# Seven small edits to a two-layer trunk kernel: decay broadcasts with 128 rows, the state chain's priority, later transposes, block-wise products, early low halves, and a shorter rstd chain

## Chip, cores and metric

One core of one Trainium2 chip. The metric is the device time of one launch in microseconds (us): the median of 3 runs, 939.8 for the kernel before (937.92 to 940.81).

## What is computed

x (512 tokens by 1024, float32) goes through two layers, each with a norm ahead of and behind it:

```python
def rmsnorm(x, g):
    return x * lax.rsqrt(jnp.mean(x * x, -1, keepdims=True) + EPS) * g

def ssd_fox_layer(x, ...):                      # layer 0
    proj = rmsnorm(x, g_pre) @ w_in
    z, xbc, dt_raw, q, k, v, f_raw = jnp.split(proj, ...)
    xbc = silu(causal_depthwise_conv(xbc, conv_w, conv_b))
    y = ssd_chunked(xs, softplus(dt_raw + dt_bias), a, bm, cm) + xs * d_skip
    yg = y * silu(z_ssd)                        # 4 groups, each normed for itself
    y = yg * lax.rsqrt(jnp.mean(yg * yg, -1, keepdims=True) + EPS) * ssd_norm
    o = forgetting_attention(q, k, v, log_sigmoid(f_raw + fgate_b)) * silu(z_fox)
    out = concatenate([y, o]) @ w_out
    return x + rmsnorm(out, g_post)

def conformer_conv_layer(x, ...):               # layer 1
    val, gate, z = jnp.split(rmsnorm(x, g_pre) @ w_in, 3, -1)
    h = causal_depthwise_conv(val * sigmoid(gate), conv_w, conv_b)   # width 31
    h = silu(layernorm(h, ln_g, ln_b)) * silu(z)
    return x + rmsnorm(h @ w_out, g_post)
```

`ssd_chunked` works on chunks of 128 tokens. Within a chunk it needs, for each of 16 heads, the decay matrix exp(cs[l] - cs[s]) under the diagonal, where cs is a running sum; between chunks a state H is carried: H = H * decay + new.

## The kernel before

The 512 tokens lie in four blocks of 128 (`NB`), the 1024 channels in eight slices of 128 (`KT`). Every product is made in three passes in a rounded float32 format: both factors are split into a high and a low half, and high x high, high x low and low x high are summed in one PSUM bank (`mm3`, or three `mm` in a row). Names with h and l at the end (`uh`, `ul`, `hlh`, `hll`) are such halves.

The work is a list of `Job`s, one for each weight tile of 128 x 1024 values. A job's weights are loaded on SyncE's queue (L163), cast on ScalarE (L157, L159) and their low half is made on VectorE or GpSimd (L191). Then `run` makes the job's products in eight chunks (a few have more). Between chunks it lets `Steps.chunk` put in steps of the state space part and of the attention: each step has a name, what it needs, and a delay in estimated microseconds (`DL`) after that. So **TensorE's order is fixed by hand**, when the program is built. On the other engines a scheduler sets the order by priority; `tc.high_priority(offset=HP)` pulls a piece of code ahead.

Part of layer 1's low halves is made ahead, during layer 0: `early` is a generator over 52 of layer 1's jobs. For each it loads the weights (`pre`, L202), casts them on ScalarE in two halves (`prh`, L211), subtracts on VectorE (`pre`, L212) and writes the low half to memory (`lo`, L216), all on the same queues. `run` advances it at each 8th chunk of jobs 5 to 12, each 7th from job 26, and each 11th from job `JO` = 56, where layer 0's output projection begins; `J1` = 72 is layer 1's first job. What isn't done by then is drained afterwards.

The places that the change touches:

- `rstd_of` (L344) makes var = ss/n + EPS on VectorE (L346) and rstd = var^-0.5 on GpSimd (L348). `sumsq` (L355) is the sum of squares, on ScalarE. `scaled` (L358) norms a block: two sums of squares, an addition (L364), rstd, and two products (L367); its result `u` is transposed on TensorE (`uT`, L106).
- `z_ssd` and `v_proj` are the products of the gate and of the attention's values: for each k a loop over the token blocks (bank names `tm`).
- the output projection (bank `o`, `first` and `second` for the two halves of 512 columns), and `finish` for each block: the sum of squares of the second half, a product with the gain (L710), the sum of both halves' squares (L711), rstd, and x + y * rstd (L714).
- the decay broadcasts: `seg` multiplies a selector, one column broadcast to 128, by the running sums `cs2` and so spreads one head's row over 128 partitions (`bc`). There are 16, four in each group. `cs2` has 48 rows: the high half in rows 0 to 15, the low half in rows 32 to 47, the rest zero.
- the state chain: `states` (the three states H of a group, L1313 and L1314) and `state_parts` (their halves, `hlh` and `hll` out of `H`, L119), which the products with the state (`yo`) need.
- `to_yT`: the transposes of a group's normed y (`yT`, L106). They come `DL[11]` after `gate_scale`, which scales y by its rstd (L1388). `cv` (L528) is the short convolution's steps, on VectorE too.

Of the kernel before, what the change touches and what calls it, by code (L numbers as in the profile page):

```python
# [15 lines left out]
P = 128  # L16
# [20 lines left out]
def trunk(  # L37
# [292 lines left out]
    def run(n, after=None):  # L330

        for _ in range(n):
            for c, _ in enumerate(chunks()):
                if after is not None:
                    after()
                i = state["run"]
                if 5 <= i < 13 or 26 <= i:
                    if (8 * i + c) % (11 if i >= JO else 7 if i >= 26 else 8) == 0:
                        next(early, None)
# [4 lines left out]
    def rstd_of(ss, n):  # L344
        v = col("var", ss.shape[-1])
        V.tensor_scalar(v, ss, 1.0 / n, EPS, ALU.mult, ALU.add)  # L346
# [10 lines left out]

    def scaled(dst, xs):  # L358

        s2 = col("s2", 2)  # L360
        for i, t in enumerate(xs):
            sumsq(t, s2[:, i : i + 1])
        if len(xs) == 2:
            V.tensor_tensor(s2[:, 0:1], s2[:, 0:1], s2[:, 1:2], ALU.add)  # L364
        r = rstd_of(s2[:, 0:1], D)
# [175 lines left out]
    def z_ssd(ch):  # L541
        pbs = []

        def go(k2, wh, wl):
            if k2 == 0:
                pbs.extend(bank("tm") for _ in range(NB))
            for j in range(2):
                k = 2 * k2 + j
                for b in range(NB):
# [13 lines left out]
    def v_proj(ch):  # L563
        pbs = []

        def go(k4, wh, wl):
            if k4 == 0:
                pbs.extend(bank("tm") for _ in range(2))
            for j in range(4):
                k = 4 * k4 + j  # L570
                for b in range(NB):
# [60 lines left out]
    def out_proj(w, stages, nk, gpost, resid, done, hooks):  # L632
# [27 lines left out]
        def first(k2, wh, wl):  # L660
# [4 lines left out]
            for j in range(2):  # L665
                k = 2 * k2 + j
                for b in range(NB):
# [3 lines left out]
                    if k == nk - 1:  # L671
                        t = t2("o0")
                        s0.append(sumsq(pb0[b]))
# [33 lines left out]
        def finish(b):  # L707
            ss = sumsq(pb1[b])
            y1 = [o0[b], t2("y1")]
            V.tensor_tensor(y1[1], pb1[b], gpost[1], ALU.mult)  # L710
            V.tensor_tensor(ss, ss, s0[b], ALU.add)  # L711
            r = rstd_of(ss, D)
# [485 lines left out]
    cs2 = cp.tile([48, S], F32R, name="cs2")  # L1198
    sel2 = cp.tile([48, 16], F32R, name="sel2")
# [3 lines left out]
    V.tensor_tensor(sel2, ident[0:48, 0:16], ident[0:48, 32:48], ALU.add)  # L1203
# [32 lines left out]
    DL = [2, 7, 4, 11, 4, 9, 4, 9, 9, 3, 3, 6]  # L1236
# [62 lines left out]
    def states(g):  # L1299
# [6 lines left out]
        H = S_["H"] = [t2("H") for _ in range(2)]  # L1306
        for c in range(3):
            h = q256(H, c)
            if c == 0:
                A.copy(h, q256(st, 0))  # L1310
            else:
                dec = cdec[:, 4 * g : 4 * g + 4, c].unsqueeze(2).to_broadcast([P, 4, 64])
                V.tensor_tensor(h4(h), h4(q256(H, c - 1)), dec, ALU.mult)  # L1313
                V.tensor_tensor(h, h, q256(st, c), ALU.add)  # L1314

    def state_parts(g):
        H = SG[g]["H"]
        r = []
        for i, w in enumerate((512, 256)):
# [282 lines left out]
```

## Time and profile before

| what | value |
|---|---|
| median of 3 runs | 939.8 us |
| the profiled execution | 940.86 us |
| its span, first to last instruction | 939.1 us |
| mean granted TensorE clock | 0.993 |
| TensorE busy | 906.6 us (97% of the span), 4683 matmuls |
| VectorE, ScalarE, GpSimd busy | 731.1, 605.3, 511.6 us |
| moved by DMA | 166.14 MB, mean 177 GB/s |

The profile shows one execution. A row of the timeline has the start, the duration, the engine (PE is TensorE, DVE VectorE, ACT ScalarE, POOL GpSimd, SPq SyncE's queue), the line, the operation, the tiles out<-in and their shape, how many rows were put together (x2), and in brackets how long the engine sat idle before it and whom it waited for. Matmuls are pipelined: each begins before the one before it has ended, so their pace is read from start to start. 128*128 ahead of a shape means rows times columns of the stationary operand. A group of a tile has count, then ns shortest/median/longest. A row of the windows has the stretch, its length, busy us (and instructions) of PE, PEld, DVE, ACT and POOL, the granted clock, the DMA share and GB/s.

### The profile page before, as it was taken

To read this page: it belongs to the slowest core of one execution; us is meant where nothing else is said; L and a number is where in the kernel's file an instruction comes from. 1 tells how busy PE (TensorE), PEld (TensorE's weight loads), DVE (VectorE), ACT (ScalarE), POOL (GpSimd) and SP (SyncE) were. 2 spreads that over 40 slices of the span, in tenths; PEclk is the share of its full clock that TensorE was granted. 3 is DMA by queue.
4 is the path that set the end of the run, shared out by engine and by line. 5 is a ranking of instruction groups with operands and counts; after the bars stand their busy time and mean duration, and the time that the engine had idled before them with its cause. 6 is when DMAs were issued, how large, how long until landed. Compare 5 with 4: busy or idle time off the path is not lost.

```text
span 939.1 us, 13909 instructions
## 1 busy us (share of the span) xinstructions
PE 906.6 (97%) x4683; PEld 755.6 (80%) x4683; DVE 731.1 (78%) x1284; ACT 605.3 (64%) x1134; POOL 511.6 (54%) x476
## 2 busy tenths in 40 slices
PE   6999999998999999989899989999999999999997
PEld 6887787787798888778678879888888887787885
DVE  5667968788977887988877347899999999979502
ACT  5757667576855767677575536987886877658300
POOL 2604554535633444445573111998999999847310
PEclk9999999999999999999999999999999999999999
DMA  7725631347765574674538986546564665554503
GB/s 208 229 77 180 202 90 53 104 128 237 241 202 159 163 243 158 182 244 150 168 110 285 333 301 227 169 157 213 180 209 150 190 197 174 157 157 155 182 1 112
DMA packets 182507, 166.14 MB, mean 177 GB/s; under 512 B 7900, under 2 KB 151908, under 8 KB 182436
## 3 DMA queue, kind: packets, MB, share of 16 engines
q1 hardware_dynamic: 182420, 165.25, 54.9%
q8 instruction: 37, 0.61, 0.3%
q14 instruction: 34, 0.28, 0.1%
q10 hardware_dynamic: 16, 0.00, 0.0%
HBM read 133.64 MB, written 31.46 MB: 176 GB/s over the span
## 4 chain that ended last, share of the span: by engine, by line
PE 42%; DVE 6%; DMA 5%; issue 2%; ACT 2%; SPq 1%; POOL 1%; DVEq 0%; POOLq 0%; ACTq 0%
PE m L102 29%; PE o L102 10%; DMA lo<-pre 3%; DVE pre L212 2%; DMA wr<-in_o_w_in_dram 1%; PE acc L102 1%; PE tm L102 1%; DMA wr<-in_e_w_out_dram 1%; DVE w L191 1%; PE s L102 1%; DVE pl L119 1%; PE pT L106 0%; DMA pre<-in_o_w_in_dram 0%; ACT pr L95 0%; DMA pre<-in_o_w_out_dram 0%
## 5 line engine op out<-in xcount | busy, mean ns | idle before, releaser
L102 PE MATMUL m<-uh,w 128*128 128x512 f32 (+1 forms) x1392 | 453.5, 393 | 0.0
L102 PEld LDWEIGHTS m<-uh,w 128*128 128x128 f32 x1392 | 261.4, 190 | 50.9 <-issue 3.1
L102 PE MATMUL m<-ul,w 128*128 128x512 f32 (+1 forms) x696 | 267.7, 385 | 0.0
L191 POOL TENSOR_TENSOR w<-wr,w 128x512 fp32r<-128x512 f32 x112 | 158.8, 1442 | 160.3 <-ACT w L159 123.6
L984 DVE SCALAR_TENSOR_TENSOR acc<-h,cw,acc 128x490 f32<-128x490 f32 (+13 forms) x274 | 179.0, 731 | 2.7 <-ACT acc L976 2.0
L891 POOL TENSOR_TENSOR acc<-acc,prod 128x507 f32<-128x507 f32 (+9 forms) x124 | 159.6, 1289 | 8.2 <-ACT prod L877 0.7
L102 PEld LDWEIGHTS m<-ul,w 128*128 128x128 f32 x696 | 132.3, 190 | 21.5 <-issue 0.5
L102 PE MATMUL o<-w,hlh 128*128 128x512 f32 x448 | 142.2, 399 | 2.3 <-ACT pr L95 2.3
L212 DVE TENSOR_TENSOR pre<-pre,prh 128x512 fp32r<-128x512 f32 x104 | 90.6, 889 | 44.8 <-ACT prh L211 44.6
L102 PEld LDWEIGHTS o<-w,hlh 128*128 128x128 f32 x448 | 83.4, 191 | 19.0 <-ACT pr L95 3.0
L102 PE MATMUL tm<-w,uh 128*128 128x256 f32 (+1 forms) x384 | 91.7, 330 | 1.9 <-ACT pr L95 0.9
L211 ACT CAST prh<-pre 128x512 fp32r<-128x512 f32 x104 | 61.2, 622 | 48.5 <-DMA pre<-in_o_w_in_dram 14.6
L1464 POOL TENSOR_SCALAR pr<-pr,ri 128x128 f32<-128x128 f32 (+1 forms) x64 | 39.7, 621 | 92.6 <-DVE ri L1463 85.8
L159 ACT CAST w<-wr 128x1024 fp32r<-128x1024 f32 x72 | 74.8, 1048 | 23.0 <-DMA wr<-in_e_w_in_dram 6.6
L102 PE MATMUL o<-w,hll 128*128 128x512 f32 x224 | 88.0, 393 | 0.0
L877 ACT ACTIVATE prod<-h,cw 128x507 f32<-128x507 f32 (+9 forms) x124 | 79.0, 709 | 0.0
L348 POOL TENSOR_TENSOR rstd<-var,mhalf 128x1 f32<-128x1 f32 (+1 forms) x20 | 14.0, 698 | 114.6 <-DVE var L346 114.6
L157 ACT CAST w<-wr 128x1024 fp32r<-128x1024 f32 x56 | 57.2, 1050 | 18.5 <-DMA wr<-in_o_w_out_dram 10.3
L102 PEld LDWEIGHTS tm<-w,uh 128*128 128x128 f32 x384 | 62.9, 190 | 7.6 <-DVE QS L605 1.1
L102 PE MATMUL tm<-w,ul 128*128 128x256 f32 (+1 forms) x192 | 61.2, 319 | 0.0
L95 ACT ACTIVATE pr<-s,nmx 128x128 f32<-128x128 f32 (+1 forms) x64 | 34.0, 531 | 38.0 <-DVE nmx L1458 27.8
L102 PEld LDWEIGHTS o<-w,hll 128*128 128x128 f32 x224 | 42.6, 190 | 9.0
(270 smaller groups left out, 1594.3 us busy)
## 6 DMA issues: line engine op xcount, KB each, us to landing
wr<-in_e_w_in_dram SPq DMA_DIRECT2D x56, 512.0 KB
lo<-pre SPq DMA_DIRECT2D x52, 512.0 KB
pre<-in_o_w_in_dram SPq DMA_DIRECT2D x48, 512.0 KB
wr<-in_o_w_in_dram SPq DMA_DIRECT2D x48, 512.0 KB
w<-lo SPq DMA_DIRECT2D x48, 512.0 KB
wr<-in_e_w_out_dram SPq DMA_DIRECT2D x16, 512.0 KB
wr<-in_o_w_out_dram SPq DMA_DIRECT2D x16, 512.0 KB
x<-in_x_dram SPq DMA_DIRECT2D x12, 256.0 KB
```

Of the source, the lines that this page charges most:

```text
L95: i = A.activation(*a, **kw)
L102: T.matmul(o, l, r, start=start, stop=stop, skip_group_check=True)
L157: last_cast[0] = A.copy(hi, src).ins
L159: last_cast[0] = A.copy(hi, src).ins
L191: j.eng.tensor_tensor(hl[1][i][:, sl], src[:, sl], f32(hl[0][i])[:, sl], ALU.subtract)
L211: A.copy(h[:, sl], t[:, sl])
L212: V.tensor_tensor(t.bitcast(F32R)[:, sl], t[:, sl], f32(h)[:, sl], ALU.subtract)
L348: mark["rstd"] = G.tensor_tensor(r, v, mhalf.to_broadcast([P, ss.shape[-1]]), ALU.pow).ins
L877: A.activation(prs[i][:, s:], hs[j][:, : S - s], AF.Copy, scale=w31(30 - s, j))
L891: G.tensor_tensor(a2[j][:, s:], a2[j][:, s:], prs.pop(i)[:, s:], ALU.add)
L984: V.scalar_tensor_tensor(a[:, s:], h[:, : S - s], w31(30 - s, j), a[:, s:], ALU.mult, ALU.add)
L1464: G.tensor_scalar(p[:, :L], p[:, :L], ri, 1.0, ALU.mult, ALU.mult)
```

## The change

1. `cs2` and `sel2` have 128 rows, the added ones zeros; the broadcast matmul uses all 128.
2. `states` and `state_parts` are pulled ahead by `high_priority`.
3. `DL[11]`, the delay ahead of a normed group's transposes, is 9 instead of 6.
4. `z_ssd`, `v_proj` and the first job of layer 0's output projection loop over token blocks outside and over k inside (`v_proj` by pairs of blocks).
5. `early` is advanced at each 7th chunk from job 26 to 69, and no more behind that.
6. In `scaled` and `finish` the first half's share of var, ss0/n + EPS, is made ahead (`part_var`), so that one instruction makes var out of the second sum of squares; in `finish` rstd is started before the product with the gain.

```diff
-                if 5 <= i < 13 or 26 <= i:
-                    if (8 * i + c) % (11 if i >= JO else 7 if i >= 26 else 8) == 0:
+                if 5 <= i < 13 or 26 <= i < J1 - 2:
+                    if (8 * i + c) % (7 if i >= 26 else 8) == 0:
                         next(early, None)
...
-    def rstd_of(ss, n):
+    def rstd_of(ss, n, pre=None):
         v = col("var", ss.shape[-1])
-        V.tensor_scalar(v, ss, 1.0 / n, EPS, ALU.mult, ALU.add)
+        if pre is None:
+            V.tensor_scalar(v, ss, 1.0 / n, EPS, ALU.mult, ALU.add)
+        else:
+            V.scalar_tensor_tensor(v, ss, 1.0 / n, pre, ALU.mult, ALU.add)
...
+    def part_var(ss, n):
+        p = col("pre")
+        V.tensor_scalar(p, ss, 1.0 / n, EPS, ALU.mult, ALU.add)
+        return p
...
-        s2 = col("s2", 2)
-        for i, t in enumerate(xs):
-            sumsq(t, s2[:, i : i + 1])
-        if len(xs) == 2:
-            V.tensor_tensor(s2[:, 0:1], s2[:, 0:1], s2[:, 1:2], ALU.add)
-        r = rstd_of(s2[:, 0:1], D)
+        pre = part_var(sumsq(xs[0]), D)
+        r = rstd_of(sumsq(xs[1]), D, pre)
...
-            for j in range(2):
-                k = 2 * k2 + j
-                for b in range(NB):
+            for b in range(NB):
+                for j in range(2):
+                    k = 2 * k2 + j
...
-            for j in range(4):
+            for b2 in range(2):
+              for j in range(4):
                 k = 4 * k4 + j
-                for b in range(NB):
+                for b in (2 * b2, 2 * b2 + 1):
...
-            for j in range(2):
-                k = 2 * k2 + j
-                for b in range(NB):
+            stagger = k2 == 0 and len(stages) == 1
+            for j, b in ((j, b) for b in range(NB) for j in range(2)) if stagger else ((j, b) for j in range(2) for b in range(NB)):
+                    k = 2 * k2 + j
...
-                        s0.append(sumsq(pb0[b]))
+                        s0.append(part_var(sumsq(pb0[b]), D))
...
             ss = sumsq(pb1[b])
+            r = rstd_of(ss, D, s0[b])
             y1 = [o0[b], t2("y1")]
             V.tensor_tensor(y1[1], pb1[b], gpost[1], ALU.mult)
-            V.tensor_tensor(ss, ss, s0[b], ALU.add)
-            r = rstd_of(ss, D)
...
-    cs2 = cp.tile([48, S], F32R, name="cs2")
-    sel2 = cp.tile([48, 16], F32R, name="sel2")
+    cs2 = cp.tile([P, S], F32R, name="cs2")
+    sel2 = cp.tile([P, 16], F32R, name="sel2")
...
-    DL = [2, 7, 4, 11, 4, 9, 4, 9, 9, 3, 3, 6]
+    DL = [2, 7, 4, 11, 4, 9, 4, 9, 9, 3, 3, 9]
...
-        H = S_["H"] = [t2("H") for _ in range(2)]
+        with tc.high_priority(offset=HP):
+            H = S_["H"] = [t2("H") for _ in range(2)]
...
-        for i, w in enumerate((512, 256)):
-            r.append(hilo(H[i][:, :w], w))
+        with tc.high_priority(offset=HP):
+            for i, w in enumerate((512, 256)):
+                r.append(hilo(H[i][:, :w], w))
...
-        mm(bc, sel2[:, h : h + 1].to_broadcast([48, P]), cs2, True, True)
+        mm(bc, sel2[:, h : h + 1].to_broadcast([P, P]), cs2, True, True)
```

How the order on the engines moves is shown at three places. First TensorE, at the transposes of group 2 (`yT`), before:

```order
L102 MATMUL m_2289<-uh_138,w_2186 128x512
L102 MATMUL m_2289<-ul_146,w_2186 128x512
L102 MATMUL m_2289<-uh_138,w_2186 128x512
L106 MATMUL yT_2299<-ident,y_1809 128x128 x2
L106 MATMUL yT_2299<-ident,y_1837 128x128 x2
L102 MATMUL m_2289<-uh_139,w_2186 128x512
```

and after, at the end of the same job's 24 matmuls:

```order
L102 MATMUL m_2297<-uh_145,w_2194 128x512
L102 MATMUL m_2297<-ul_153,w_2194 128x512
L102 MATMUL m_2297<-uh_145,w_2194 128x512
L106 MATMUL yT_2349<-ident,y_1814 128x128 x2
L106 MATMUL yT_2349<-ident,y_1833 128x128 x2
L102 MATMUL m_2367<-uh_138,w_2252 128x512
```

The job that stands as m_2289 before and as m_2297 after has 24 matmuls: the transposes stood behind its third and now stand behind its last, 21 matmuls later. In group 3 they move by 12.

Second, VectorE in front of those transposes, before:

```order
L346 TENSOR_SCALAR var_2207<-ss_2198 128x4
L212 TENSOR_TENSOR pre_2313<-pre_2313,prh_2428 128x512
L528 SCALAR_TENSOR_TENSOR cv_2177<-m_2101,c_136,cv_2177 128x509
L1388 TENSOR_SCALAR y_1809<-y_1809,rstd_2209 128x256 x2
L1388 TENSOR_SCALAR y_1837<-y_1837,rstd_2209 128x256
L528 SCALAR_TENSOR_TENSOR cv_2239<-m_2182,c_136,cv_2239 128x511
L1388 TENSOR_SCALAR y_1837<-y_1837,rstd_2209 128x256
```

and after:

```order
L347 TENSOR_SCALAR var_2230<-ss_2221 128x4
L212 TENSOR_TENSOR pre_2272<-pre_2272,prh_2356 128x512
L533 SCALAR_TENSOR_TENSOR cv_2243<-m_2190,c_136,cv_2243 128x511
L1395 TENSOR_SCALAR y_1814<-y_1814,rstd_2232 128x256
L533 SCALAR_TENSOR_TENSOR cv_2243<-m_2190,c_136,cv_2243 128x510
L1395 TENSOR_SCALAR y_1814<-y_1814,rstd_2232 128x256
L533 SCALAR_TENSOR_TENSOR cv_2243<-m_2190,c_136,cv_2243 128x509
L1395 TENSOR_SCALAR y_1833<-y_1833,rstd_2232 128x256 x2
```

Between var and the last scaling of y stood two convolution steps; now there are three, and two of them lie between the scalings. Ahead of the first group's decays and state chain, one pair of early subtractions (`pre`) fewer stands now; the low halves of the state (`hll` out of `H`) still follow those of the decays (`hll` out of `seg`).

Third, VectorE at the end of layer 0, where the last block's x is made and normed for layer 1, before:

```order
L710 TENSOR_TENSOR y_1329_6195<-o_1258_5902,x_5662 128x512
L711 TENSOR_TENSOR ss_6192<-ss_6192,ss_5881 128x1
L212 TENSOR_TENSOR pre_6102<-pre_6102,prh_6247 128x512
L346 TENSOR_SCALAR var_6198<-ss_6192 128x1
L212 TENSOR_TENSOR pre_6102<-pre_6102,prh_6247 128x512
L714 SCALAR_TENSOR_TENSOR o_1248_5880<-o_1248_5880,rstd_6200,x_6070 128x512
L714 SCALAR_TENSOR_TENSOR y_1329_6195<-y_1329_6195,rstd_6200,x_6071 128x512
```

and after:

```order
L349 SCALAR_TENSOR_TENSOR var_6228<-ss_6225,pre_5921 128x1
L717 TENSOR_TENSOR y_1350_6232<-o_1282_5954,x_5688 128x512
L719 SCALAR_TENSOR_TENSOR o_1266_5917<-o_1266_5917,rstd_6230,x_6120 128x512
L719 SCALAR_TENSOR_TENSOR y_1350_6232<-y_1350_6232,rstd_6230,x_6121 128x512
L364 TENSOR_SCALAR pre_6245<-ss_6242 128x1
L349 SCALAR_TENSOR_TENSOR var_6250<-ss_6247,pre_6245 128x1
L372 TENSOR_SCALAR u_6240<-o_1266_5917,rstd_6252 128x512
L372 TENSOR_SCALAR u_6241<-y_1350_6232,rstd_6252 128x512
```

The two early subtractions (`pre` out of `prh`) are gone from this place, and var stands ahead of the product y. (The `pre` of 128x1 is `part_var`'s result.)

More of the change, by code (lines that the diff above doesn't have):

```diff
@@ L1202, in trunk @@
     V.tensor_copy(cs2[32:48, :], f32(csl)[0:16, :])
-    V.tensor_tensor(sel2, ident[0:48, 0:16], ident[0:48, 32:48], ALU.add)
+    V.tensor_tensor(sel2, ident[:, 0:16], ident[:, 32:48], ALU.add)
     tk = cp.tile([P, NB, P], F32, name="tk")
@@ L1305, in states @@
             mm3(q256(st, c), Bth[:, tok(c)], Btl[:, tok(c)], eh, el, True, True)
-        H = S_["H"] = [t2("H") for _ in range(2)]
[L1307 to L1314, printed above, removed]
+        with tc.high_priority(offset=HP):
+            H = S_["H"] = [t2("H") for _ in range(2)]
+            for c in range(3):
+                h = q256(H, c)
+                if c == 0:
+                    A.copy(h, q256(st, 0))
+                else:
+                    dec = cdec[:, 4 * g : 4 * g + 4, c].unsqueeze(2).to_broadcast([P, 4, 64])
+                    V.tensor_tensor(h4(h), h4(q256(H, c - 1)), dec, ALU.mult)
+                    V.tensor_tensor(h, h, q256(st, c), ALU.add)
     def state_parts(g):
```

## The prediction

> **What bounds the kernel now.** I read the page first, then the waits of TensorE, then its timeline at the places where the waits lie. The page's first lines:
>
> ```profile
> span 939.1 us, 13909 instructions
> PE 906.6 (97%) x4683; PEld 755.6 (80%) x4683; DVE 731.1 (78%) x1284; ACT 605.3 (64%) x1134; POOL 511.6 (54%) x476
> ```
>
> TensorE is busy for 97% of the span, so nothing that shortens another engine counts unless a TensorE wait goes with it, or TensorE's own work gets shorter. Its waits (us in total, times, longest):
>
> ```profile
> PE uT L106 <- DVE u L367: 2.8, 1, 2.8
> PE yT L106 <- DVE y L1388: 2.6, 2, 1.6
> PE o L102 <- ACT pr L95: 2.5, 4, 0.9
> PE yo L102 <- DVE hll L119: 2.0, 2, 1.6
> PE s L102 <- ACT pr L95: 1.5, 2, 0.8
> ```
>
> The change can win back little more than these rows, the slow clock that follows a wait, and whatever TensorE does badly while it counts as busy. For the last, the starts in the timeline matter, not the durations, since matmuls overlap. Around one decay broadcast:
>
> ```profile
> 145.26 0.40 PE L102 MATMUL m<-uh,w 128*128 128x512 f32 x1
> 145.59 0.49 PE L102 MATMUL bc<-cs,sel 48*128 48x512 f32 x1
> 146.01 0.50 PE L102 MATMUL m<-uh,w 128*128 128x512 f32 x1
> 146.34 0.40 PE L102 MATMUL m<-ul,w 128*128 128x512 f32 x1
> 146.58 0.40 PE L102 MATMUL m<-uh,w 128*128 128x512 f32 x1
> ```
>
> Start to start: 0.33 into the broadcast, 0.42 out of it, 0.33 to the next, then 0.24. Undisturbed, a 512-column matmul starts 0.23 after the one before it: the fourth interval here has just recovered, and two that are counted in one row last 0.62 where one lasts 0.39 (the rows at 567.24 and 220.99 further on). The first three intervals hold 0.33 + 0.42 + 0.33 - 3 x 0.23 = 0.39 too much.
>
> **The decay broadcasts with 128 rows.** The new rows are zeros, so the columns that stream (512) stay the same, and the evacuation reads the same bank. What must be judged is whether the 48 rows are what costs. A matmul that also leaves rows out, in the attention:
>
> ```profile
> 420.18 0.34 PE L102 MATMUL s<-KS,QS 128*128 128x384 f32 x1
> 420.36 0.34 PE L102 MATMUL s<-KX,QX 68*128 68x384 f32 x1
> 420.54 0.23 PE L102 MATMUL s<-maskq,identb 128*128 128x128 bf16 x1
> ```
>
> From 128 rows to 68 takes 0.18 and back 0.18, which is the pace for 384 columns (384/512 x 0.23 = 0.17). [...]
>
> ```profile
> L102 PE MATMUL bc<-cs,sel 48*128 48x512 f32 x16 | 7.9, 492 | 0.0
> ```
>
> Sixteen broadcasts x 0.39 = **6.2**. The two intervals next to the broadcast alone would give 16 x 0.29 = 4.6. [...]
>
> **State chain ahead.** The wait at the first group's products with the state:
>
> ```profile
> 107.59 0.28 PE L102 MATMUL yo<-hlh,hlh 128*128 128x256 f32 x1
> 109.47 0.39 PE L102 MATMUL yo<-hll,hlh 128*128 128x256 f32 x1 [1.60 <-DVE hll L119]
> ...
> 102.58 1.76 DVE L212 TENSOR_TENSOR pre<-pre,prh 128x512 fp32r<-128x512 f32 x1
> 107.66 3.17 DVE L119 TENSOR_TENSOR hll<-H,hlh 128x512 fp32r<-128x512 f32 x2
> ```
>
> The low half of the state starts at 107.66 and TensorE waits 1.60 here, 2.0 in all by the row above. In the changed order it still stands behind the four low halves of the decays, with two early subtractions among them as before; a pair of early subtractions that stood ahead of them is gone from the place, between 2 x 0.69 (a row below) and 2 x 1.76. But TensorE reaches its products 4 x 0.39 = 1.6 sooner, because of the group's four broadcasts, and only in part do the decays come sooner with it. I take half, **1.0**; ends 0 and 2.0.
>
> **Normed group's transposes later.** Group 2:
>
> ```profile
> 220.99 0.39 PE L102 MATMUL m<-uh,w 128*128 128x512 f32 x1
> 222.99 0.76 PE L106 MATMUL yT<-ident,y 128*128 128x128 f32 x3 [1.61 <-DVE y L1388]
> 224.70 0.33 PE L106 MATMUL yT<-ident,y 128*128 128x128 f32 x1 [0.95 <-DVE y L1388]
> 226.02 0.78 PE L102 MATMUL m<-uh,w 128*128 128x512 f32 x1
> ...
> 229.43 0.63 PE L102 MATMUL m<-uh,w 128*128 128x512 f32 x2
> ...
> 223.29 0.74 DVE L528 SCALAR_TENSOR_TENSOR cv<-m,c,cv 128x511 f32<-128x511 f32 x1
> ```
>
> Waits 1.61 + 0.95 = 2.56. Between 226.02 and 229.43 eight matmuls start, which is 3.41 where 8 x 0.23 = 1.84, so a half-speed clock costs another 1.57; together 4.1. The order puts the transposes 21 matmuls later, 21 x 0.23 = 4.8. VectorE's scaling now has one convolution step more in front of its last instruction, 0.74, so 2.56 + 0.74 = 3.3 must be covered and 4.8 is there. I take **4.0**; ends 2.0 (the chain a further 3.6 late) and 4.1. [...] The rows show half speed straight behind both waits, so I count it.
>
> In group 3 the transposes move 12 matmuls, 2.7, and the two low halves of a weight now stand ahead of its rstd on GpSimd:
>
> ```profile
> L191 POOL TENSOR_TENSOR w<-wr,w x112: 1276/1302/2762, 24.2 to 896.6; 128x512 fp32r<-128x512 f32 x112
> ```
>
> That is 2 x 1.3 = 2.6 against 2.7. There was no wait there before, so I allow **-1.0** for this and for other new short waits; ends 0 and -2.0.
>
> **Early low halves ended sooner, rstd chain shorter.** At the end of layer 0:
>
> ```profile
> 557.05 0.69 DVE L212 TENSOR_TENSOR pre<-pre,prh 128x512 fp32r<-128x512 f32 x1 [4.75 <-ACT prh L211]
> 557.66 0.15 DVE L346 TENSOR_SCALAR var<-ss 128x1 f32<-128x1 f32 x1
> ...
> 562.67 2.29 PE L106 MATMUL uT<-ident,u 128*128 128x128 f32 x14 [2.81 <-DVE u L367]
> 564.61 1.20 PE L102 MATMUL o<-w,hlh 128*128 128x512 f32 x2
> ...
> 567.24 0.62 PE L102 MATMUL o<-w,hlh 128*128 128x512 f32 x2
> ```
>
> In front of var stood an early subtraction that waited for its cast and its load: 4.75 + 0.69 lost on the chain that ends in u. With the 52 early jobs done before, the chain starts about 5.4 sooner and has 2.81 to cover. Also gone is the slow clock behind it: 6 matmuls from 564.61 to 567.24 take 2.63 instead of 1.38, 1.25. Together **4.1**; next late is the residual's load, which now has no early store behind it. Ends 2.8 and 4.7 (the transposes run slowly too). The early steps before that come closer together in the output projection (each 7th chunk, not each 11th): four of the 52 jobs move ahead, 4 x 1.05 MB, at
>
> ```profile
> 530.00:545.00 15.00, 15.00 (x68) 12.42 (x67) 3.35 (x6) 5.76 (x12) 0.00 (x0) 1.00 0.95 335
> ```
>
> 335 GB/s and a share of 0.95 that makes 12.5 later for whatever is queued behind. The last weight was cast at 524.5 and used at 539.8, 15.3 of cover:
>
> ```profile
> L159 ACT CAST w<-wr x6: 1046/1048/1055, 500.6 to 524.5; 128x1024 fp32r<-128x1024 f32 x6
> 539.76 0.62 PE L102 MATMUL o<-w,hlh 128*128 128x512 f32 x2
> ```
>
> So nothing, and at most a wait of 3 if the stores delay the queue by another 6. In the attention (waits of 2.5 and 1.5 above, behind the exponentials on ScalarE), there is one more pair of early casts in the order, while the staggered first job gives the exponentials room: I take **+1.0**, ends -2 and +4 (all of both rows).
>
> At the very end:
>
> ```profile
> 933.82 0.15 DVE L346 TENSOR_SCALAR var<-ss 128x1 f32<-128x1 f32 x1
> 934.12 0.55 POOL L348 TENSOR_TENSOR rstd<-var,mhalf 128x1 f32<-128x1 f32 x1 [6.29 <-DVE var L346]
> 934.70 0.75 DVE L714 SCALAR_TENSOR_TENSOR o<-o,rstd,x 128x512 f32<-128x512 f32 x1 [0.72 <-POOL rstd L348]
> ```
>
> Until now the post-norm product (0.69) and the addition (0.15) stand ahead of var. When var goes first, rstd runs beside the product: **0.8** off the tail. The start has the same shorter chain, but there the next weights set the pace, so I count 0. The products taken block by block change no count of matmuls, and they free banks one by one: 0.
>
> **The sum.** 6.2 + 1.0 + 4.0 + 4.1 + 1.0 + 0.8 - 1.0 = 16.1. The profiled execution took 940.86, of which the span is 939.1 and 1.8 lies outside it; the median of the runs is 939.8. I go from 940.3, midway: **924.2**.
>
> **The rivals.**
>
> *Rows don't matter* (the broadcast operand costs). The broadcasts keep their 6.2: 924.2 + 6.2 = 930.4. For it: the stationary stays a broadcast of one column. Against it: the interval before the broadcast is long too. Chance 0.10.
>
> *The attention is bound by VectorE and ScalarE.* Time won before it is lost again in waits for banks, and only the boundary and the tail stay, 4.1 + 0.8: 940.3 - 4.9 = 935.4. For it: the two rows on pr. Against it: 1.5 + 2.5 is little, and TensorE would have to wait three times as much there. Chance 0.13.
>
> *Slower: the block order asks for weights too early.* With the token block outside, the second k of a gate job's weight tile is needed after 3 matmuls, not after 12: 9 x 0.23 = 2.1 sooner. The value jobs need their fourth k 18 half-width matmuls sooner, again 2.1. If each of the 16 jobs waits for that, 16 x 2.1 = 33 is lost: 924.2 + 33 = 957; from 8 such jobs on (8 x 2.1 = 16.8) the gain is gone. Tightest is the first of these jobs:
>
> ```profile
> 45.10 0.62 PE L102 MATMUL tm<-w,uh 128*128 128x512 f32 x2
> 42.47 2.98 POOL L191 TENSOR_TENSOR w<-wr,w 128x512 fp32r<-128x512 f32 x2 [0.53 <-ACT w L159]
> ```
>
> GpSimd ends at 45.45, the low half is needed at about 46. For the others no TensorE wait names a weight. Chance 0.03.
>
> *The state chain isn't ahead:* its 1.0 is lost, 925.2; a case inside the forecast, 0.1 of its chance.
>
> **How the numbers follow.** The forecast has 0.70, the rivals 0.10, 0.13 and 0.03; 0.04 is left for other losses that bring it to no change. The range reaches up to 936, over the first two rivals, and down to 917: with every term at its better end (6.2 + 2.0 + 4.1 + 4.7 + 4.0 + 0.8, no allowance) the sum is 21.8, 918.5, and one more stretch of slow clock as long as the 1.57 above, behind a wait of the attention, may go too. About 0.3% (2.8) can be told from no change; 935.4 is beyond that. Faster 0.92, same 0.04, slower 0.04.
>
> **What would show it.** Right: m to bc to m at 0.23 each; no yT and uT rows among the waits, no matmul at half speed near 227 and 565; var directly behind the last sum of squares at the end of layer 0, and o on VectorE 0.8 closer to the last matmul. Wrong: broadcasts with the same 0.33 and 0.42; waits for pr above 8 in the sum; waits of tm for w.

## The result, and the profile after

The changed kernel takes 933.6 us (median of 8 runs, 931.1 to 936.9) where the kernel before took 939.8 in the same set of runs (937.1 to 944.1): a ratio of 0.9935, 95% interval 0.9913 to 0.9956. So it is faster, by 6.2 and not by the 16 that were forecast. The profiled execution of the changed kernel took 932.8, span 931.0; against the profiled execution before (span 939.1) that is 8.1. Of the runs of all kernels told here one is left out of the medians and ranges: 1115.1 of the version nohp_dl6, at a granted clock of 0.75.

The page's first lines, then TensorE's waits (us in total, times, longest), in the changed kernel:

```profile
span 931.0 us, 13931 instructions
PE 899.8 (97%) x4683; PEld 755.9 (81%) x4683; DVE 727.0 (78%) x1284; ACT 605.2 (65%) x1134; POOL 513.8 (55%) x476
```

```profile
PE yd L102 <- DVE hll L119: 3.2, 2, 1.7
PE m L102 <- DVE y L1277: 1.3, 1, 1.3
PE yT L106 <- DVE y L1395: 0.6, 1, 0.6
PE st L102 <- POOL hll L119: 0.6, 1, 0.6
PE yo L102 <- DVE hll L119: 0.4, 1, 0.4
```

The wait of uT for u (2.8) is gone and that of yT is down from 2.6 to 0.6. New rows stand in their place: yd, the products with the decays, waits 3.2 for their low halves, and m and st wait too. None of these three rows was among the waits before.

The broadcasts did what the forecast said. The group by tile and the timeline around one:

```profile
L102 PE MATMUL bc<-cs,sel x16: 388/393/397, 83.7 to 240.8; 128*128 128x512 f32 x16
```

```profile
142.85 0.40 PE L102 MATMUL m<-uh,w 128*128 128x512 f32 x1
143.09 0.39 PE L102 MATMUL bc<-cs,sel 128*128 128x512 f32 x1
143.32 0.39 PE L102 MATMUL m<-uh,w 128*128 128x512 f32 x1
143.55 0.39 PE L102 MATMUL m<-ul,w 128*128 128x512 f32 x1
```

0.24 into the broadcast, 0.23 out of it, 0.23 to the next: the 0.39 is gone at each of the 16, though a wait of another cause stands behind one of them. A broadcast lasts 393 ns where it was 491. The tail came out as forecast too. From the last matmul to the second half's o on VectorE it was 934.70 - 931.84 = 2.86 and is 926.65 - 924.62 = 2.03, so 0.83 less. The last matmul before, then the tail after:

```profile
931.84 0.39 PE L102 MATMUL o<-w,hll 128*128 128x512 f32 x1
```

```profile
924.62 0.39 PE L102 MATMUL o<-w,hll 128*128 128x512 f32 x1
...
925.76 0.16 DVE L349 SCALAR_TENSOR_TENSOR var<-ss,pre 128x1 f32<-128x1 f32 x1 [4.51 <-ACT junk L358]
925.84 0.69 DVE L717 TENSOR_TENSOR y<-o,x 128x512 f32<-128x512 f32 x1
926.65 0.75 DVE L719 SCALAR_TENSOR_TENSOR o<-o,rstd,x 128x512 f32<-128x512 f32 x1
```

And at the end of layer 0, TensorE is busy for all of the stretch in which it lost 2.8 before (the columns are PE, PEld, DVE, ACT, POOL, clock, DMA share, GB/s):

```profile
545.00:565.00 20.00, 20.00 (x114) 17.48 (x113) 10.41 (x27) 8.34 (x25) 2.21 (x4) 1.00 0.90 305
```

**Where the time went.** Put the start of the same TensorE work in both traces side by side, changed minus before. The n-th matmul of a tile is the same work in both. The steps stand among other products than before, so a single difference is good to 1 or 2 us:

| place in the program | before | changed | difference |
|---|---|---|---|
| group 0's first broadcast | 84.26 | 83.74 | -0.5 |
| group 1's first broadcast | 145.59 | 143.09 | -2.5 |
| group 2's first broadcast | 180.93 | 176.82 | -4.1 |
| group 3's first broadcast | 244.04 | 235.85 | -8.2 |
| first value job of the next chain (tm, 193rd of w,uh) | 296.74 | 294.94 | -1.8 |
| output projection, 129th of o<-w,hlh | 518.00 | 515.71 | -2.3 |
| first matmul of layer 1 | 567.93 | 560.99 | -6.9 |
| last matmul | 931.84 | 924.62 | -7.2 |

Up to group 3 the forecast had 12 x 0.39 for the broadcasts, 1.0 and 4.0, together 9.7, and most of it is there: 8.2 by 236. Then 6.4 of it is given back between 236 and 295. There, in the changed kernel:

```profile
256.27 0.28 PE L102 MATMUL yd<-hll,hlh 128*128 128x64 f32 x1
258.09 0.30 PE L102 MATMUL yd<-hlh,hll 128*128 128x64 f32 x1 [1.54 <-DVE hll L119]
```

```profile
252.00:256.00 4.00, 4.00 (x36) 4.00 (x36) 3.43 (x4) 4.00 (x8) 2.93 (x3) 1.00 0.26 77
256.00:260.00 4.00, 2.46 (x16) 2.35 (x15) 3.90 (x7) 2.68 (x7) 1.49 (x2) 0.80 0.50 153
260.00:264.00 4.00, 4.00 (x20) 4.00 (x20) 2.68 (x5) 3.00 (x5) 0.28 (x1) 0.50 0.75 290
264.00:268.00 4.00, 4.00 (x31) 4.00 (x31) 3.79 (x5) 0.91 (x3) 2.68 (x2) 0.85 0.88 247
```

A wait of 1.54, and behind it 6.83 us at half clock, from 258.38 to 265.21 (0.80, 0.50 and 0.85 in the rows above). Three matmuls of the values take 0.64 there (260.80 to 261.44) where they took 0.36 (250.27 to 250.63). The clock costs (0.20 + 0.50 + 0.15) x 4 = 3.4; with the waits of m (1.3) and st (0.6) just before, 1.5 + 3.4 + 1.3 + 0.6 = 6.8. The four broadcasts of this group save 1.6 in the same stretch, so the 6.4 net is a loss of 8.0, and about 1.2 of it has no row here. VectorE shows why the low halves are late:

```profile
226.02 2.86 DVE L212 TENSOR_TENSOR pre<-pre,prh 128x512 fp32r<-128x512 f32 x2
229.57 1.62 DVE L212 TENSOR_TENSOR pre<-pre,prh 128x512 fp32r<-128x512 f32 x2 [0.69 <-ACT prh L211]
235.00 1.29 DVE L212 TENSOR_TENSOR pre<-pre,prh 128x512 fp32r<-128x512 f32 x2 [3.81 <-ACT prh L211]
236.21 0.68 DVE L119 TENSOR_TENSOR hll<-xt,hlh 128x512 fp32r<-128x512 f32 x1
...
244.09 0.34 DVE L1354 SCALAR_TENSOR_TENSOR seg<-bc,tk,maskT 128x128 f32<-128x128 f32 x1
```

Three pairs of early subtractions stand ahead of group 3's first step, and the third waits 3.81 for its cast. On ScalarE that cast waits for its load:

```profile
234.35 1.14 ACT L211 CAST prh<-pre 128x512 fp32r<-128x512 f32 x2 [1.69 <-DMA pre<-in_o_w_in_dram]
235.39 1.06 ACT L118 CAST hlh<-xt 128x512 fp32r<-128x512 f32 x2
```

TensorE came to this group's broadcasts 8.2 sooner than before, but VectorE turned to the decays of group 3 at 244.09, where it was 244.57 before. Half a microsecond is all that the chain moved at this step. VectorE there before:

```profile
244.57 1.13 DVE L1347 SCALAR_TENSOR_TENSOR seg<-bc,tk,maskT 128x128 f32<-128x128 f32 x4
```

### The profile page after: what moved, and what is told of

Same layout as the page of the kernel before. It is cut to its first block, busy times and chain, and to the rows that moved or that the text cites. A ratio compares the mean times of both kernels' runs of the same rounds, so it can differ in the third digit from the quotient of the medians.

```text
span 931.0 us, 13931 instructions
## 1 busy us (share of the span) xinstructions
PE 899.8 (97%) x4683; PEld 755.9 (81%) x4683; DVE 727.0 (78%) x1284; ACT 605.2 (65%) x1134; POOL 513.8 (55%) x476
## 4 chain that ended last, share of the span: by engine, by line
PE 51%; DVE 4%; issue 1%; DMA 1%; ACT 1%; POOL 0%; DVEq 0%; POOLq 0%; ACTq 0%
PE m L102 30%; PE o L102 18%; DVE pre L212 1%; PE acc L102 1%; PE tm L102 1%; PE s L102 1%; DVE pl L119 1%; DMA pre<-in_o_w_in_dram 1%; PE pT L106 1%; DVE nmx L1465 0%; DVE w L191 0%; DMA lo<-pre 0%; PE uT L106 0%; DVE KX L624 0%; DVE cvo L1087 0%
## 5 line engine op out<-in xcount | busy, mean ns | idle before, releaser
L191 POOL TENSOR_TENSOR w<-wr,w 128x512 fp32r<-128x512 f32 x112 | 161.1, 1462 | 165.8 <-ACT w L159 130.6
L102 PE MATMUL o<-w,hlh 128*128 128x512 f32 x448 | 140.1, 394 | 0.8 <-ACT pr L95 0.8
```

The costliest lines, as they stand in the source:

```text
L102: T.matmul(o, l, r, start=start, stop=stop, skip_group_check=True)
L191: j.eng.tensor_tensor(hl[1][i][:, sl], src[:, sl], f32(hl[0][i])[:, sl], ALU.subtract)
```

## The experiments

Theory 1 is that group 3 gives the time back, because early pairs in the queues of ScalarE and VectorE hold its chain. Its rivals: the state chain's priority did it; VectorE is simply full there; each part of the change adds by itself, and the missing time is elsewhere. Medians of 4 to 12 runs, with the lowest and highest run, and the ratio to the kernel before on the same chip. The kernel before took 939.8 beside the changed kernel and 940.2 to 941.5 beside the others, so differences between rows are good to about 2 us, besides the spread of the runs:

| kernel | median us | lowest to highest | ratio (95%) |
|---|---|---|---|
| changed kernel | 933.6 | 931.1 to 936.9 | 0.9935 (0.9913 to 0.9956) |
| bc48 | 934.3 | 931.2 to 937.8 | 0.9936 (0.9917 to 0.9955) |
| pause_early | 926.8 | 924.8 to 927.7 | 0.9853 (0.9838 to 0.9868) |
| dl6 | 933.0 | 930.7 to 935.6 | 0.9923 (0.9906 to 0.9939) |
| old_early | 935.6 | 934.0 to 940.4 | 0.9949 (0.9934 to 0.9964) |
| bc_only | 940.6 | 937.8 to 945.4 | 0.9991 (0.9968 to 1.0015) |
| no_hp | 926.5 | 923.8 to 929.5 | 0.9840 (0.9807 to 0.9874) |
| pause_b | 946.2 | 941.6 to 948.6 | 1.0044 (1.0019 to 1.0069) |
| pause2 | 923.7 | 922.1 to 925.0 | 0.9807 (0.9776 to 0.9838) |
| hp_not2 | 924.2 | 923.5 to 926.3 | 0.9818 (0.9794 to 0.9842) |
| nohp_bc48 | 928.9 | 927.9 to 930.4 | 0.9868 (0.9847 to 0.9888) |
| nohp_old_early | 928.4 | 926.8 to 928.7 | 0.9857 (0.9834 to 0.9880) |
| nohp_pause2 | 923.3 | 922.9 to 924.7 | 0.9809 (0.9787 to 0.9832) |
| nohp_dl6 | 934.0 | 932.6 to 936.1 | 0.9932 (0.9906 to 0.9958) |
| nohp_old_rstd | 926.6 | 924.7 to 930.7 | 0.9857 (0.9831 to 0.9883) |
| nohp_old_loops | 928.5 | 926.2 to 929.5 | 0.9866 (0.9840 to 0.9892) |

### The broadcasts taken back

```diff
-    cs2 = cp.tile([P, S], F32R, name="cs2")
+    cs2 = cp.tile([48, S], F32R, name="cs2")
...
-        mm(bc, sel2[:, h : h + 1].to_broadcast([P, P]), cs2, True, True)
+        mm(bc, sel2[:, h : h + 1].to_broadcast([48, P]), cs2, True, True)
```

> The changed kernel with the decay broadcasts back at 48 rows. Theory 1, group 3 gives back: in the changed kernel TensorE reaches group 3's broadcasts 8.2 us sooner than before, but VectorE's work on them starts at the same time as before (244.1 against 244.6), and the waits and the slow clock between 240 and 268 give about 6 back. With 48 rows TensorE arrives there only 3.3 sooner, and the waits there mostly vanish. So the 6.5 of the broadcasts is lost and about 4 to 5 of it comes back in group 3: about 935.5 (934 to 937) where the changed kernel has 933.6. Rival, each part adds by itself: 933.6 + 6.5 = 940. Trace, both: intervals of 0.33 and 0.42 around each broadcast; theory 1 alone: no half clock near 260.

Measured 934.3, 0.7 more than the changed kernel. The edit that saves TensorE 6.2 is worth next to nothing in the changed kernel. The rival that parts add (940) falls. TensorE came to group 3's broadcasts 2.6 later than in the changed kernel (238.49 beside 235.85), not the 4.9 that was expected, and the wait in group 3 stayed. So that part of theory 1's expectation (no half clock near 260) was wrong: the clock fell to 0.81 between 260 and 264 in this run too. The mean granted clock of these runs was higher, though: 0.9965 in the median, 0.993 in the changed kernel. By an estimate from these two, up to 0.0035 x 934 = 3.3 of what the broadcasts save went to the slow clock in the changed kernel.

### The early pairs paused in group 3

```diff
-                if 5 <= i < 13 or 26 <= i < J1 - 2:
-                    if (8 * i + c) % (7 if i >= 26 else 8) == 0:
+                if 5 <= i < 13 or 26 <= i < 28 or 34 <= i < J1 - 2:
+                    if (8 * i + c) % (6 if i >= 44 else 5 if i >= 34 else 7 if i >= 26 else 8) == 0:
```

> The changed kernel, but the early low halves stand still in jobs 28 to 33 (the stretch of group 3's decay and state chain) and are made up for behind it (each 5th chunk in jobs 34 to 43, then each 6th). Theory 1, the early pairs (load, cast, subtraction) that stand in ScalarE's and VectorE's queues ahead of group 3's chain hold it at its old time: VectorE's chain moves up by 4 or more, the waits at 240, 245 and 258 and the half clock behind them go, about 5 us less than the changed kernel: 928.6 (927 to 931). Rival, the state chain's priority puts the decays' low halves of group 3 late: no change, 933.6. Rival, VectorE is simply full there: gain below 1.5, 932 or more.

Measured 926.8, 6.8 less than the changed kernel. TensorE keeps its lead through group 3: at the 193rd tm it is 9.7 ahead of the kernel before, where the changed kernel was 1.8 ahead, and the clock between 252 and 260 is 1.00. Group 3's first step on VectorE starts at 227.62, where the changed kernel has 236.21. VectorE was not full (it sat idle for 3.81 in the rows above); it stood behind work that waited.

### The transposes back at their old place

```diff
-    DL = [2, 7, 4, 11, 4, 9, 4, 9, 9, 3, 3, 9]
+    DL = [2, 7, 4, 11, 4, 9, 4, 9, 9, 3, 3, 6]
```

> The changed kernel with DL[11] back at 6, so the normed groups' transposes stand where they stood. Theory 1: the waits at group 2's transposes return (2.5 us net in the trace pair), but TensorE reaches group 3 that much later, so group 3 gives that much less back: no change, 933.6 (932.6 to 934.8). Rival, each part adds by itself: 933.6 + 2.5 = 936.1, or 4 with the whole of the old wait, 937.6.

Measured 933.0, no change. The waits at group 2's transposes came back (4.2 in all, the longest 3.2, with half clock from 220.84 to 227.66), and the wait and slow clock in group 3 went: they are one wait that moves.

### The early low halves advanced as before

```diff
-                if 5 <= i < 13 or 26 <= i < J1 - 2:
-                    if (8 * i + c) % (7 if i >= 26 else 8) == 0:
+                if 5 <= i < 13 or 26 <= i:
+                    if (8 * i + c) % (11 if i >= JO else 7 if i >= 26 else 8) == 0:
```

> The changed kernel with the early low halves advanced as before (each 11th chunk in the output projection, no end at job 70). Behind the layer boundary nothing gives time back (the difference of the two traces stays at 6.9 to 7.2 from there to the end), so both theories expect the whole of it: the wait of 2.8 and the slow clock behind it return, 933.6 + 4.6 = 938.2 (937 to 939). If the shorter rstd chain alone makes the boundary: below 935.

Measured 935.6, 2.0 more and not 4.6. The profiled run shows the wait back at the boundary (2.3 for u, and 1.4 for uh behind it); that run was the slowest of its six.

### 128 rows in the kernel before, alone

```diff
-    cs2 = cp.tile([48, S], F32R, name="cs2")
-    sel2 = cp.tile([48, 16], F32R, name="sel2")
+    cs2 = cp.tile([P, S], F32R, name="cs2")
+    sel2 = cp.tile([P, 16], F32R, name="sel2")
...
-        mm(bc, sel2[:, h : h + 1].to_broadcast([48, P]), cs2, True, True)
+        mm(bc, sel2[:, h : h + 1].to_broadcast([P, P]), cs2, True, True)
```

> The kernel before with 128 rows in the decay broadcasts and nothing else. The broadcasts themselves save 16 x 0.40 = 6.4 of TensorE's time, both theories say so. Theory 1: each group's chain on VectorE does not move up with TensorE, so group 0's wait for the state grows by 1.6, group 2's wait for its transposes by some 3, and group 3 waits a little: 1 to 2.5 is left at the end, 938.5 (937 to 939.5, before 940.2). Rival, each part adds by itself: 940.2 - 6.4 = 933.8. Trace: no interval of 0.42 behind a broadcast in either case.

Measured 940.6 beside 940.6. The gain is less than theory 1 expected, and clearly not the 6.4 that TensorE saved. Where it went, first in group 0 and then in group 2 (timeline of TensorE in this kernel):

```profile
109.34 0.38 PE L102 MATMUL yo<-hll,hlh 128*128 128x256 f32 x1 [2.91 <-DVE hll L119]
...
223.20 0.91 PE L106 MATMUL yT<-ident,y 128*128 128x128 f32 x3 [3.92 <-DVE y L1388]
```

Group 0's wait grew from 1.60 to 2.91, and group 2's from 1.61 to 3.92. Behind group 2's wait the first two 512-column matmuls start 0.58 apart (225.03 and 225.61), where 0.23 is undisturbed, which I read as the slow clock. VectorE is ready at 109.34 and 223.20, and was at 109.47 and 222.99. The runs agree: their mean granted clock is 0.987 in the median of 12, and 0.994 in the 23 runs of the kernel before beside them. A saving on TensorE ahead of such a wait made the wait longer here, and the slow clock with it.

### Without the state chain's priority

```diff
-        with tc.high_priority(offset=HP):
-            H = S_["H"] = [t2("H") for _ in range(2)]
...
+        H = S_["H"] = [t2("H") for _ in range(2)]
...
-        with tc.high_priority(offset=HP):
-            for i, w in enumerate((512, 256)):
-                r.append(hilo(H[i][:, :w], w))
+        for i, w in enumerate((512, 256)):
+            r.append(hilo(H[i][:, :w], w))
```

> The changed kernel without the priority of the state chain (states and state_parts as before). Theory 1: the low halves of the state stand behind those of the decays with it and without it, so at most group 0 moves by a microsecond, and group 3 takes that back: 933.6 (932.5 to 935). Rival, the priority is what makes the new wait of 1.7 in group 0 and that of 1.7 in group 3 with its slow clock: without it the time falls by 3 or more, to 930.

Measured 926.5, 7.1 less than the changed kernel: here my theory's number was wrong and the rival's right. This one edit cost more than any other brought, but for the transposes further on. VectorE in this kernel, at the place shown above:

```profile
224.03 2.86 DVE L212 TENSOR_TENSOR pre<-pre,prh 128x512 fp32r<-128x512 f32 x2
228.17 3.38 DVE L212 TENSOR_TENSOR pre<-pre,prh 128x512 fp32r<-128x512 f32 x2 [1.28 <-ACT prh L211]
231.47 0.68 DVE L119 TENSOR_TENSOR hll<-xt,hlh 128x512 fp32r<-128x512 f32 x1
```

Two pairs of early subtractions stand there, not three, and group 3's first step comes at 231.47, not 236.21. The order shows where the third went: without the priority it stands in group 2's stretch, among the state chain and its sums. Ahead of group 2's low halves of the state stand 22 early subtractions, 20 with the priority; ahead of group 3's first step it is 42 in both. The two theories are one: the early pairs hold group 3, and the priority put one more of them there.

### The priority in all groups but the second

```diff
-        with tc.high_priority(offset=HP):
+        with tc.high_priority(offset=HP if g != 2 else 0):
```

(in `states` and in `state_parts`)

> The changed kernel with the state chain's priority in groups 0, 1 and 3, but not in group 2. Theory: the priority in group 2 pushes one early pair from group 2's state into the queue ahead of group 3's first products (three pairs of early subtractions stand there in the changed kernel, two without the priority), and that pair, waiting for its load, holds group 3's chain. Then leaving group 2 out is enough: 926.5 (925 to 928.5), as without any priority, and no half clock near 260. Rival, the priority in group 3 or 0 itself makes the new waits: 932 to 934.

Measured 924.2, as expected or a little better. VectorE has two pairs ahead of group 3's first step again:

```profile
224.51 2.85 DVE L212 TENSOR_TENSOR pre<-pre,prh 128x512 fp32r<-128x512 f32 x2
228.65 3.36 DVE L212 TENSOR_TENSOR pre<-pre,prh 128x512 fp32r<-128x512 f32 x2 [1.29 <-ACT prh L211]
231.94 0.68 DVE L119 TENSOR_TENSOR hll<-xt,hlh 128x512 fp32r<-128x512 f32 x1
```

No wait and no half clock stands between 236 and 290. It is the priority in group 2 that does the harm, in group 3.

### The pause in the kernel before

```diff
-                if 5 <= i < 13 or 26 <= i:
-                    if (8 * i + c) % (11 if i >= JO else 7 if i >= 26 else 8) == 0:
+                if 5 <= i < 13 or 26 <= i < 28 or 34 <= i:
+                    if (8 * i + c) % (9 if i >= JO else 6 if i >= 34 else 7 if i >= 26 else 8) == 0:
```

> The kernel before with the early low halves paused in jobs 28 to 33 and made up behind (each 6th chunk from job 34, each 9th in the output projection). Theory 1: before, TensorE does not wait in group 3, so nothing is to be won there: 940 (938.5 to 941), where the same pause in the changed kernel won 6.8. Rival, the pause is worth its 6.8 wherever it is made: 933.4.

Measured slower, ratio 1.0044. The pause isn't worth its 6.8 wherever it is made, but "nothing is to be won there" was wrong too. By the middle of the first value job (the 145th tm) it had won 5.1, since group 2's wait for its transposes was gone; early subtractions ahead of it had been a part of it. It lost 3.2 of that in the attention, with two stretches of 6.83 at half clock where the kernel before has one of 3.41, and more at the layer boundary, since the early jobs ended later:

```profile
564.59 3.12 PE L106 MATMUL uT<-ident,u 128*128 128x128 f32 x14 [6.65 <-DVE u L367]
```

6.65 where it was 2.81. The early pairs must stand somewhere, and the question is what waits behind them.

### Paused in group 0 as well, with the priority and without it

```diff
-                if 5 <= i < 13 or 26 <= i < J1 - 2:
-                    if (8 * i + c) % (7 if i >= 26 else 8) == 0:
+                if 5 <= i < 9 or 26 <= i < 28 or 34 <= i < J1 - 2:
+                    if (8 * i + c) % (6 if i >= 55 else 5 if i >= 34 else 7 if i >= 26 else 6) == 0:
```

> The changed kernel with the early low halves paused in group 3's stretch, and in group 0's too: each 6th chunk in jobs 5 to 8, none in 9 to 25, each 7th in 26 and 27, none in 28 to 33, each 5th from 34 to 54, each 6th to 69. Theory 1: group 0's waits (1.85 and 0.78 in the changed kernel) are made by early subtractions ahead of the decays' low halves, and with group 3 paused nothing gives the gain back: 926.8 - 2.5 = 924.3 (923 to 926). If group 0 is bound by VectorE's own work: 926.8. If the attention, with more early pairs, takes it back: 927 or more, with more waits for pr between 390 and 460.

> Without the state chain's priority, and with the early low halves paused in both groups' stretches, as in the run that paused them twice. Theory: both remove the same wait in group 3, so they don't add; the pause in group 0 still removes its waits: 923.7 (922 to 925.5), as with the priority. Rival, the two are separate causes: 923.7 - 7 = 917.

Measured 923.7 and 923.3. No wait of yd or yo in group 0 is left, and the pause and the priority's removal don't add, since both take away the same wait. These two, with the priority out of group 2 alone (924.2), are the fastest versions here: about 10 below the changed kernel, and 17 to 18 below the kernel before beside them.

### Each other part taken back, without the priority

The edits are those above (48 rows; the old advance; `DL[11]` of 6), and two more, the rstd chain and the loops as before:

```diff
-            r = rstd_of(ss, D, s0[b])
             y1 = [o0[b], t2("y1")]
             V.tensor_tensor(y1[1], pb1[b], gpost[1], ALU.mult)
+            V.tensor_tensor(ss, ss, s0[b], ALU.add)
+            r = rstd_of(ss, D)
```

```diff
-            for b in range(NB):
-                for j in range(2):
-                    k = 2 * k2 + j
+            for j in range(2):
+                k = 2 * k2 + j
+                for b in range(NB):
...
-            stagger = k2 == 0 and len(stages) == 1
+            stagger = False
```

(the rstd edit also in `scaled` and where `s0` is made, the loop edit also in `v_proj`)

> Without the state chain's priority, and the decay broadcasts at 48 rows. Theory: without the late chain in group 3 nothing gives time back there, so the broadcasts' whole 6.5 is lost, less what group 0's wait (2.3 and 0.8 without the priority) gives: 926.5 + 5 to 6.5 = 931.5 to 933. Rival, the broadcasts save nothing that lasts, as in the changed kernel, where going back to 48 rows cost 0.7: 926.5 to 927.5.

> Without the state chain's priority, and the early low halves advanced as before. Theory: the wait and slow clock at the layer boundary return, 926.5 + 4.6 = 931.1 (930 to 932). If the shorter rstd chain makes most of the boundary's gain: 926.5 + 2 or less, as the medians of the changed kernel with the old advance suggested (935.6 beside 933.6).

> Without the state chain's priority, and DL[11] back at 6. Theory: nothing behind takes the time back now, so the waits at group 2's transposes cost what they show there, 2.5 to 4 (in the changed kernel, with group 3 held, going back cost nothing: 933.0 beside 933.6): 926.5 + 3.3 = 929.8 (929 to 930.5) by the median. Rival, the transposes' wait was only ever moved, not removed: 926.5 to 927.5.

> Without the state chain's priority, and with the rstd chain as before (sums added first, the product with the gain ahead of var). The tail is the end of the program, so its 0.8 is lost whole; elsewhere the chain is covered: 926.5 + 0.8 = 927.3 (927 to 928.3). Trace: 0.84 more between the last matmul and the last o on VectorE.

> Without the state chain's priority, and the products' loops as before (k outside, token blocks inside, no staggered first job). Prediction's term: 0, 926.5 (925.5 to 927.5). If the stagger gives the attention's exponentials room at the start of the output projection: 1 to 3 more, with more waits for pr between 440 and 460. If the group of gate products frees its banks sooner in block order: more waits at 104 to 111, 1 to 2.

Against 926.5: the broadcasts 2.4 (expected 5 to 6.5), the early end 1.9 (expected 4.6), the transposes 7.5 (expected 3.3), the rstd chain 0.1 (expected 0.8), the loops 2.0 (expected 0). Runs of one kernel spread over 2 to 6 us here, so of these only the transposes are clear; the others are within about what these runs can tell apart, and I read them as small, not as measured to the microsecond. The trace does have the rstd chain's 0.84 at the tail (2.87 from the last matmul to the last o on VectorE, and 2.03 with the short chain). The transposes were worth nearly twice the 4.0 forecast. Between group 2's first broadcast and group 3's the trace loses 7.1 against the kernel without the priority; waits of 3.36 and 0.8 and slow clock of 3.4 (6.83 at half) stand there:

```profile
223.82 0.91 PE L106 MATMUL yT<-ident,y 128*128 128x128 f32 x3 [3.36 <-DVE y L1393]
```

3.36 where the kernel before waited 1.61: TensorE stands there at 220.5, and stood there at 221.4 before; VectorE's scaling is ready at 223.8, and was at 223.0.

## Why the prediction was wrong

**The step that failed is "State chain ahead", priced at 1.0 with ends 0 and 2.0.** I read the order only at the first group, where the priority moves little, and left out a loss. The runs put it at a loss of 7.1 by the medians, 8.9 by the ratios: without the priority the change takes 926.5 (ratio 0.984, so 15 of 940). In group 0 the priority does bring a part of what was forecast: the waits there are 1.69 + 0.44 = 2.13 with it and 0.62 + 2.17 = 2.79 without it, 0.7 less. But what it takes ahead of the early pairs in group 2 it puts in front of group 3. There one more pair waits for its load (1.69 on ScalarE, 3.81 on VectorE), group 3's casts and subtractions stand behind it, and 6.4 of a lead of 8.2 is given back. The term "-1.0 for new short waits" is where that should have been. I bounded it by GpSimd's two low halves in group 3, which were not the cause.

That the other terms of the sum promise 16.1 - 1.0 = 15.1, and 15 came without the priority, is partly luck: taken back one by one the terms measured 2.4, 7.5, 1.9, 0.1 and 2.0, other than they were priced.

The order shown ahead of the prediction was read too simply as well. It says that one pair of early subtractions fewer stands ahead of the first group's decays and state chain. In the traces 18 early subtractions stand ahead of that group's low halves of the state in both kernels, and ahead of its first decay step 14 in the changed kernel and 11 before: they moved, and none is gone.

**Broadcasts, 6.2:** the cost was right to the interval (0.39 each, gone with 128 rows), and the rival that rows don't matter is refuted. Why 48 rows cost it and 68 nothing, no run shows. What stays at the end is another matter: 0.0 alone in the kernel before, 0.7 in the changed kernel, 2.4 without the priority. I had counted the whole, and had asked only in group 0 whether VectorE's chain comes sooner with TensorE. At each place where TensorE waits for such a chain, the sum of all gains up to there has to be compared with the slack.

**Transposes, 4.0:** the waits went as forecast (2.56 to 0.6, and no half speed behind: the clock is 1.00 up to 258.38). Without the priority the edit is worth 7.5 (7.1 in the trace): more than its own 4.0. As in bc_only, the wait and the slow clock there are longer when TensorE comes to them sooner. With the priority it is worth 0.

**Boundary, 4.1:** the wait and the slow clock are gone, 4.6 in the trace pair between 518 and the first matmul of layer 1. Taking the edit back costs 1.9 to 2.0 by the medians, while the profiled runs lose 5.2 (with the priority) and 5.0 (without it) from the 129th matmul of the output projection to the end. In the pair without the priority 1.2 of that is balanced by chance: that kernel's profiled run was at half clock from 448.75 to 452.17, and the one with the old advance was not. The rest of the difference stays open; one execution of each was profiled, and that of old_early was its slowest. By the medians alone the other case of that expectation, that the shorter rstd chain makes most of this gain (926.5 + 2), would fit. The traces speak for the early low halves: with the old rstd chain no wait stands at the boundary, with the old advance one of 2.3 for u or, without the priority, of 1.9 for uh.

**Tail, 0.8:** 0.83 in the trace. **Attention, +1.0:** 0.5 in the trace, from 295 to 518. Luck has a part in it: the profiled run of the kernel before was at half clock there for 3.41, that of the changed kernel was not. **Block order, 0:** 2.0 worth, unclear. The waits for pr add up to 3.6 with the old loops and 3.8 with the new, so they don't explain it; those of group 0's products with the state are 2.91 + 0.45 with the old loops, 2.17 with the new. No wait of tm for a weight appeared, so the slower rival had no ground. **The rival that the attention takes it back** named the right way to lose, a wait that grows as TensorE gains, but the wrong place. The give-back was in the state space part, group by group.

The range held the time (933.6 in 917 to 936), but only because it reached to that rival; the sum itself was 9.4 off, and the direction right. (The chances of the forecast and its first two rivals add up to 0.93, where 0.92 is written.)

## What to carry to other kernels

A microsecond saved on the bounding engine counts only up to the next place where that engine waits for a chain that doesn't move with it. Add up the gains ahead of each such place and compare the sum with the slack there. Background work that shares an engine's queue with urgent chains needs a place where nothing urgent stands behind it. A priority that pulls one chain ahead of it can move it in front of the next chain, as it did here.

## What the runs showed of the hardware

**The slow clock isn't settled by the length of a wait alone.** The same wait of 2.17 at the same place (group 0's products with the state) in two kernels, without the priority and the same with `DL[11]` of 6. Timeline of TensorE, then the windows behind it, first without the priority:

```profile
109.11 0.39 PE L102 MATMUL yo<-hll,hlh 128*128 128x256 f32 x1 [2.17 <-DVE hll L119]
```

```profile
112.00:116.00 4.00, 4.00 (x23) 3.47 (x23) 3.96 (x7) 2.47 (x4) 0.00 (x0) 1.00 0.02 6
```

and with the old delay:

```profile
109.25 0.39 PE L102 MATMUL yo<-hll,hlh 128*128 128x256 f32 x1 [2.17 <-DVE hll L119]
```

```profile
112.00:116.00 4.00, 4.00 (x17) 3.65 (x16) 3.34 (x7) 1.75 (x2) 0.00 (x0) 0.50 0.03 7
```

The clock stayed at 1.00 in one and fell to 0.50 in the other, which cost 3.2 (the 200th matmul of m<-uh,w starts 3.36 later, where the place itself was 0.14 later). All 17 traces show a common pattern. Until the end of the program their clock is 1.00 or 0.50, each stretch at 0.50 lasts 3.41 or 6.83, and each change lies a whole number of 3.41 behind the first record at 1.00, which falls anywhere from 11.08 to 16.04 (14.18 in the kernel before, 12.62 in the changed kernel). Cut each trace into pieces of 3.41 along its own grid, and take the pieces at full clock: where TensorE sat idle for 1.95 or more in one piece, a piece at half clock followed in 12 of 12 cases; between 1.05 and 1.95 in 20 of 67; below 1.05 in none of 4390 (in the kernel before and the changed kernel together 1 of 1, 3 of 11 and none of 518). Of the two waits of 2.17 above, the first has 1.69 in one piece (the grid cuts it at 107.42), the second 1.92 (cut at 107.33). Both lie in the middle range. That the place of the grid made the difference fits these numbers, but it is my estimate, which two cases don't show. A piece at half clock costs up to 0.5 x 3.41 = 1.7, by an estimate from these numbers, so this is also a reason why runs of one kernel spread over 2 to 8 us: the fastest run of nohp_old_rstd (924.7) had a mean granted clock of 0.999, the slowest (930.7) 0.993.

**Rows of the stationary operand.** A matmul of 48 rows between matmuls of 128 cost 0.39 more than one of 128 rows that holds the same values and zeros (0.33, 0.42 and 0.33 from start to start in the kernel before, and 0.24, 0.23 and 0.23 in the changed kernel). 68 rows cost nothing: there 384 columns take 0.18 from start to start, from 128 rows to 68 and from 68 on, and the pace of 512 columns gives 384/512 x 0.23 = 0.17. Where between 48 and 68 rows the cost begins, and what makes it, was not measured.
